# Pads of 64 bytes before and behind the pool of small tiles, in a two-block decoder kernel

## The chip, the cores and the metric

The kernel runs on one core of a Trainium2 chip. The metric is device time of one execution in microseconds; the median of several runs is compared. All inputs lie in the chip's main memory as float32 and are laid out by the host before the launch.

## The reference

Two transformer blocks over 256 tokens of width 1024, batch 1, all in float32. What matters here is that nearly all of it is matrix products, and that the largest part is the expert layer at the end of the second block:

```python
def second_block(x, mem, ...):
    ...
        x = x + peer_ffn(h, peer_w_q[l], peer_subkeys[l], peer_w_down[l], peer_w_up[l])
    return rmsnorm(x, final_g)

def peer_ffn(h, w_q, subkeys, w_down, w_up):
    ...
        q = (xc @ w_q).reshape(PEER_TOK_CHUNK, PEER_HEADS, 2, half).astype(jnp.float32)
        s = jnp.einsum("thpd,hpnd->thpn", q, subkeys.astype(jnp.float32))
        ...
        top_s, top_pos = lax.top_k(cand_s, PEER_TOPK)
        e = jnp.take_along_axis(cand_i, top_pos, axis=-1)
        g = jax.nn.softmax(top_s, axis=-1).astype(xc.dtype)
        a = jax.nn.gelu(jnp.einsum("td,thkd->thk", xc, w_down[e]))
        return jnp.einsum("thk,thkd->td", g * a, w_up[e])
```

Ahead of it stand the first block (a gated recurrence, a multi-scale pooling, a merge, a squared-ReLU MLP of width 4096, two layer norms) and the second block's attention, spatial gating and cross attention. There are 16,384 experts, so w_down and w_up of the expert layer are 64 MB each.

## The kernel before

**Products in split precision.** Every large product is done in float32r with both operands split in a high and a low part, and three matmuls for each pair: high x high, low x high, high x low. Two functions do nearly all of them. gemm_t (lines 195 to 223) keeps a 128x128 slice of the weights stationary and moves 256 columns of activations (all tokens), which gives a transposed result; its three matmuls are lines 207, 208 and 209. gemm_n (lines 226 to 296) keeps a 128x128 slice of the activations stationary (one half of the tokens) and moves 512 columns of weights, which gives a result with tokens on the partitions; its matmul is line 240.

**Weights.** They come as 128x1024 pieces (512 KB) by DMA, issued on SyncE's queue in one fixed order (`plan`), into tiles named raw. feed (line 134) makes the high part with ScalarE (line 152), low (line 159) the low part with VectorE (line 164: raw minus high). A piece with both parts is a tile w of pool spl (4 buffers, line 144), or wb in pool big, or a part of lend.

**The expert layer.** It computes all experts densely, in 16 groups of 1024. down(g) is a gemm_t of w_down with the normalised input h4, followed by a gelu into slots. route (line 1306) makes, from the routing weights, one-hot tables (tile oo, VectorE, lines 1330 to 1333), multiplies them on TensorE (tile gt, line 1339) and scales the activations in slots (line 1343). up(g, ...) (line 1373) multiplies the scaled activations with w_up into four PSUM banks py, which are kept over all 16 groups:

```python
            for n, (x, w) in enumerate(((wh, hi), (wl, hi), (wh, lo))):
                for h in which:
                    PE.matmul(yps[t][h], x[:, i % 2, tok(t)], w[:, h * 512:h * 512 + 512], ...
```

The stationary operand is a 128x128 slice of wh or wl, the moving one 512 columns of a weight piece. wh and wl are the split parts of two rows of slots, made by halves (line 1351) through split_to (lines 316 and 317).

**Where tiles lie.** Tiles are placed by pool, in the order in which pools are opened, each start rounded up to 32 bytes of the partition:

| pool, line | tiles that matter | first byte | start modulo 256 |
|---|---|---|---|
| keep, 36 | xh/xl, x1, h2, h3, h4 (high and low, 8192 bytes each) | 18,048 | 128 |
| raw, 37 | raw | 34,432 | 128 |
| sm, 38 | all of t2 (2048 bytes each), among them wh and wl; small statistics | 50,816 | 128 |
| spl, 42 | w | 67,392 | 64 |
| big, 46 | wb, and activations such as f0h to f3l, mh, ml, oh, ol; later lend and slots | 100,160 | 64 |

Slices that the matmuls use start at multiples of 512 bytes within a tile, so a slice has the residue of its tile.

**What sets the order.** TensorE, VectorE and ScalarE run in the order of the source; side work (the recurrence, attention, routing) is put between steps of the products by generators. The last pool's last tile, rt, ends at byte 229,184 of 229,376.

Of the kernel before, what the change touches and what calls it, by code (L numbers as in the profile page):

```python
# [8 lines left out]
F32 = mybir.dt.float32  # L9
# [8 lines left out]
P = 128  # L18
# [12 lines left out]
def kernel(ctx: ExitStack, tc: tile.TileContext, A: dict, out: bass.AP):  # L31
    nc = tc.nc
    V, S, G, PE = nc.vector, nc.scalar, nc.gpsimd, nc.tensor

    const = ctx.enter_context(tc.tile_pool(name="const", bufs=1))
    keep = ctx.enter_context(tc.tile_pool(name="keep", bufs=1))
    raw_p = ctx.enter_context(tc.tile_pool(name="raw", bufs=4))
    sm = ctx.enter_context(tc.tile_pool(name="sm", bufs=2))
    ps_n = ctx.enter_context(tc.tile_pool(name="ps_n", bufs=4, space=bass.MemoryType.PSUM))
    ps_p = ctx.enter_context(tc.tile_pool(name="ps_p", bufs=2, space=bass.MemoryType.PSUM))  # L40
    ps_s = ctx.enter_context(tc.tile_pool(name="ps_s", bufs=2, space=bass.MemoryType.PSUM))
    spl = ctx.enter_context(tc.tile_pool(name="spl", bufs=4))
    dram = ctx.enter_context(tc.tile_pool(name="dram", bufs=1, space=bass.MemoryType.DRAM))
    phase = ctx.enter_context(ExitStack())
# [1528 lines left out]
```

## Time and profile before

| | us |
|---|---|
| median of 3 runs | 1504.67 (1504.32 to 1505.53) |
| the profiled execution | 1504.66 |
| its span, first to last instruction | 1502.9 |
| TensorE busy with matmuls, of the span | 1465.1 |
| VectorE busy | 1084.0 |
| ScalarE busy | 714.4 |

The order of time is: first block to about 430 us, second block's mixer and cross attention to about 700 us, then the expert layer: down of 14 groups to 1071 us (with the routing beside it), up of two groups with the last two downs to 1161 us, up of the others to 1487 us, with the second routing beside it until about 1304 us, and a tail. A matmul's recorded length is longer than the time to the next one, since matmuls overlap; how often one starts is read from a stretch and its count.

### The profile page before, as it was taken

To read this page: it belongs to the slowest core of one execution; us is meant where nothing else is said; L and a number is where in the kernel's file an instruction comes from. 1 tells how busy PE (TensorE), PEld (TensorE's weight loads), DVE (VectorE), ACT (ScalarE), POOL (GpSimd) and SP (SyncE) were. 2 spreads that over 40 slices of the span, in tenths; PEclk is the share of its full clock that TensorE was granted. 3 is DMA by queue.
4 is the path that set the end of the run, shared out by engine and by line. 5 is a ranking of instruction groups with operands and counts; after the bars stand their busy time and mean duration, and the time that the engine had idled before them with its cause. 6 is when DMAs were issued, how large, how long until landed. Compare 5 with 4: busy or idle time off the path is not lost.

```text
span 1502.9 us, 25892 instructions
## 1 busy us (share of the span) xinstructions
PE 1465.1 (97%) x10408; PEld 1325.0 (88%) x10408; DVE 1084.0 (72%) x1932; ACT 714.4 (48%) x929; POOL 37.6 (3%) x70
## 2 busy tenths in 40 slices
PE   8999999999999999899999999999999999999997
PEld 8989997998877898778999999999999777788885
DVE  6876787565488679545998966888645999855555
ACT  5663354454453565444544544434444444444443
POOL 1004000000001000000000000000000000000001
PEclk9999999999999999999999999999999999999999
DMA  8554574466645455424456555555566555556552
GB/s 287 176 160 123 156 242 177 172 208 196 196 170 197 137 183 160 168 68 169 155 167 212 183 185 182 164 160 169 169 184 195 158 180 192 174 183 194 187 186 90
DMA packets 72761, 263.41 MB, mean 175 GB/s; under 512 B 8240, under 2 KB 8752, under 8 KB 72128
## 3 DMA queue, kind: packets, MB, share of 16 engines
q1 hardware_dynamic: 70416, 252.48, 52.7%
q0 software_dynamic: 1936, 8.98, 1.6%
q8 instruction: 82, 1.34, 0.4%
q14 instruction: 39, 0.32, 0.1%
q10 hardware_dynamic: 288, 0.30, 0.1%
HBM read 259.62 MB, written 2.10 MB: 174 GB/s over the span
## 4 chain that ended last, share of the span: by engine, by line
PE 93%; DVE 5%; ACT 1%; DMA 1%; issue 0%; SPq 0%; ACTq 0%; DVEq 0%
PE py L1381 24%; PE pt L207 16%; PE pt L208 16%; PE pn L240 16%; PE pt L209 16%; PE gt L1339 2%; DVE wb L164 1%; PE hs L625 1%; PE sk L1264 0%; DVE w L164 0%; PE tr L332 0%; PE tr L454 0%; DMA raw<-in_xa_o_dram 0%; DMA raw<-in_w_f_dram 0%; DVE rs_a L400 0%
## 5 line engine op out<-in xcount | busy, mean ns | idle before, releaser
L152 ACT ACTIVATE w<-raw 128x1024 fp32r<-128x1024 f32 (+1 forms) x416 | 436.1, 1050 | 583.6 <-PE pt L209 276.5
L164 DVE TENSOR_TENSOR w<-raw,w 128x1024 fp32r<-128x1024 f32 x410 | 499.0, 1221 | 168.6 <-ACT w L152 168.0
L207 PE MATMUL pt<-h4h,w 128*128 128x256 f32 x1088 | 307.4, 283 | 0.0
L208 PE MATMUL pt<-h4l,w 128*128 128x256 f32 x1088 | 304.6, 280 | 0.0
L209 PE MATMUL pt<-h4h,w 128*128 128x256 f32 x1088 | 303.7, 279 | 0.0
L1381 PE MATMUL py<-w,wh 128*128 128x512 f32 x1024 | 289.1, 398 | 0.0
L1381 PEld LDWEIGHTS py<-w,wh 128*128 128x128 f32 x1024 | 189.9, 188 | 43.4
L207 PEld LDWEIGHTS pt<-h4h,w 128*128 128x128 f32 x1088 | 204.7, 188 | 0.1
L208 PEld LDWEIGHTS pt<-h4l,w 128*128 128x128 f32 x1088 | 204.3, 188 | 0.1
L209 PEld LDWEIGHTS pt<-h4h,w 128*128 128x128 f32 x1088 | 203.7, 187 | 0.0
L1381 PE MATMUL py<-w,wl 128*128 128x512 f32 x512 | 161.5, 395 | 0.0
L1381 PEld LDWEIGHTS py<-w,wl 128*128 128x128 f32 x512 | 96.2, 188 | 22.9
L207 PE MATMUL pt<-xh,w 128*128 128x256 f32 x384 | 110.6, 288 | 5.3 <-ACT w L152 5.3
L209 PE MATMUL pt<-xh,w 128*128 128x256 f32 x384 | 108.7, 283 | 0.0
L208 PE MATMUL pt<-xl,w 128*128 128x256 f32 x384 | 108.7, 283 | 0.0
L317 DVE TENSOR_TENSOR wl<-slots,wh 128x512 fp32r<-128x512 f32 (+1 forms) x68 | 44.3, 658 | 80.7 <-ACT wh L316 80.7
L207 PEld LDWEIGHTS pt<-xh,w 128*128 128x128 f32 x384 | 73.2, 191 | 5.9 <-ACT w L152 5.6
L152 ACT ACTIVATE wb<-raw 128x1024 fp32r<-128x1024 f32 x62 | 62.8, 1048 | 33.0 <-DMA raw<-in_w_up_dram 10.5
L164 DVE TENSOR_TENSOR wb<-raw,wb 128x1024 fp32r<-128x1024 f32 x62 | 73.4, 1218 | 2.2 <-ACT wb L152 2.0
L208 PEld LDWEIGHTS pt<-xl,w 128*128 128x128 f32 x384 | 73.3, 191 | 0.4 <-DVE xl L317 0.2
L209 PEld LDWEIGHTS pt<-xh,w 128*128 128x128 f32 x384 | 73.1, 190 | 0.1
L1333 DVE TENSOR_TENSOR oo<-oo,rt 128x512 f16<-128x512 f16 x128 | 48.7, 421 | 2.2
(488 smaller groups left out, 2415.1 us busy)
## 6 DMA issues: line engine op xcount, KB each, us to landing
raw<-in_peer_down_dram SPq DMA_DIRECT2D x128, 512.0 KB, 3.6
raw<-in_peer_up_dram SPq DMA_DIRECT2D x128, 512.0 KB, 3.7
raw<-in_w_up_dram SPq DMA_DIRECT2D x32, 512.0 KB, 4.8
raw<-in_w_down_dram SPq DMA_DIRECT2D x32, 512.0 KB, 3.8
raw<-in_w_gb_dram SPq DMA_DIRECT2D x16, 512.0 KB, 4.0
raw<-in_w_ga_dram SPq DMA_DIRECT2D x16, 512.0 KB, 4.7
raw<-in_w_out_dram SPq DMA_DIRECT2D x16, 512.0 KB, 4.5
raw<-in_peer_q_dram SPq DMA_DIRECT2D x16, 512.0 KB, 5.0
```

Source lines behind the costliest of these rows:

```text
L152: S.activation(pc[:, 0, x], raw[:, x], AF.Copy)
L164: V.tensor_tensor(pc[:, 1, :], raw, f32(pc[:, 0, :]), OP.subtract)
L207: PE.matmul(o, hi[:, f:f + P], xh(b, k, ALL), start=(k == 0), stop=False)
L208: PE.matmul(o, hi[:, f:f + P], xl(b, k, ALL), start=False, stop=False)
L209: PE.matmul(o, lo[:, f:f + P], xh(b, k, ALL), start=False, stop=(k == nk - 1))
L240: PE.matmul(o, xx(k, t), ww[:, kk * n + h * 512:kk * n + h * 512 + 512], start=(k == 0 and i == 0), stop=(k == nk - 1 and i == 2))
L317: V.tensor_tensor(lo, src, f32(hi), OP.subtract)
L625: PE.matmul(ps[:, h, :], kk[:, h, tok(t)], qq[:, h, tok(t)], start=True, stop=True)
L1333: V.tensor_tensor(o2[:, i].rearrange("p t (a two) -> p t a two", two=2), q2, turn(1 + i, t0, n), OP.mult)
L1339: PE.matmul(ps[:, u, :], p1[:, u, :], p2[:, i, u, :], start=(i == 1), stop=(i == 2))
L1381: PE.matmul(yps[t][h], x[:, i % 2, tok(t)], w[:, h * 512:h * 512 + 512], start=(first and i == 0 and n == 0), stop=(last and i == 7 and n ...
```

## The change

Two tiles of 16 float32 per partition (64 bytes), edge and edge2, are placed in pools of their own, one between the pools raw and sm, one between sm and spl. Each is filled with zeros by a memset on GpSimd, and nothing reads it.

```diff
     raw_p = ctx.enter_context(tc.tile_pool(name="raw", bufs=4))
+    edge = ctx.enter_context(tc.tile_pool(name="edge", bufs=1)).tile([P, 16], F32, tag="edge", name="edge")
+    G.memset(edge, 0.0)
     sm = ctx.enter_context(tc.tile_pool(name="sm", bufs=2))
     ps_n = ctx.enter_context(tc.tile_pool(name="ps_n", bufs=4, space=bass.MemoryType.PSUM))
     ps_p = ctx.enter_context(tc.tile_pool(name="ps_p", bufs=2, space=bass.MemoryType.PSUM))
     ps_s = ctx.enter_context(tc.tile_pool(name="ps_s", bufs=2, space=bass.MemoryType.PSUM))
+    edge2 = ctx.enter_context(tc.tile_pool(name="edge2", bufs=1)).tile([P, 16], F32, tag="edge2", name="edge2")
+    G.memset(edge2, 0.0)
     spl = ctx.enter_context(tc.tile_pool(name="spl", bufs=4))
```

So sm moves by 64 bytes and every pool behind it by 128; keep and raw stay. Modulo 256, before and after:

| pool | before | after |
|---|---|---|
| keep (activations of the products) | 128 | 128 |
| sm (wh, wl among them) | 128 | 192 |
| spl, big (weights, other activations) | 64 | 192 |

The order of instructions is the same on every engine but GpSimd, where the two memsets stand ahead of the one of ident. GpSimd's program before, from the branch into the kernel on (ident is the identity matrix for transposes, epsb and iof are constants):

```order
L1569 UNCONDITIONAL_BRANCH
L383 MEMSET ident 128x128
L387 MEMSET epsb 128x1
L389 ISA
L389 IOTA iof 128x128
L384 AFFINE_SELECT ident<-ident 128x128
```

The same place after the change:

```order
L1573 UNCONDITIONAL_BRANCH
L39 MEMSET edge 128x16
L45 MEMSET edge_84 128x16
L387 MEMSET ident 128x128
L391 MEMSET epsb 128x1
L393 ISA
L393 IOTA iof 128x128
L388 AFFINE_SELECT ident<-ident 128x128
```

All that GpSimd does after the branch stands two instructions later; nothing else has moved.

## Rows read from the trace of the kernel before

**Rows 1.** The page: busy time of the engines, and the chain by line.

```profile
PE 1465.1 (97%) x10408; PEld 1325.0 (88%) x10408; DVE 1084.0 (72%) x1932; ACT 714.4 (48%) x929; POOL 37.6 (3%) x70
...
PE 93%; DVE 5%; ACT 1%; DMA 1%; issue 0%; SPq 0%; ACTq 0%; DVEq 0%
PE py L1381 24%; PE pt L207 16%; PE pt L208 16%; PE pn L240 16%; PE pt L209 16%; PE gt L1339 2%; DVE wb L164 1%; PE hs L625 1%; PE sk L1264 0%; DVE w L164 0%; PE tr L332 0%; PE tr L454 0%; DMA raw<-in_xa_o_dram 0%; DMA raw<-in_w_f_dram 0%; DVE rs_a L400 0%
```

**Rows 2.** Waits: total us, times, longest.

```profile
ACT w L152 <- PE py L1381: 178.4, 114, 2.6
```

**Rows 3.** Stretches: us, busy time and instructions by engine, clock, DMA share, GB/s.

```profile
core 0: us, PE busy (x) PEld busy (x) DVE busy (x) ACT busy (x) POOL busy (x), PEclk, DMA share, GB/s
346.00:429.00 83.00, 83.00 (x368) 68.73 (x367) 46.39 (x52) 37.89 (x39) 0.00 (x0) 1.00 0.67 209
691.00:696.00 5.00, 5.00 (x23) 4.05 (x22) 2.13 (x4) 3.23 (x5) 0.00 (x0) 1.00 0.94 338
742.00:823.00 81.00, 81.00 (x690) 81.00 (x689) 76.75 (x261) 41.78 (x50) 0.00 (x0) 1.00 0.59 186
202.00:223.00 21.00, 21.00 (x177) 21.00 (x176) 20.80 (x24) 14.14 (x17) 0.73 (x1) 1.00 0.86 300
1164.00:1304.00 140.00, 140.00 (x1024) 110.79 (x1023) 134.97 (x250) 58.11 (x66) 1.05 (x2) 1.00 0.54 174
1308.00:1487.00 179.00, 179.00 (x775) 144.30 (x772) 97.01 (x99) 83.22 (x96) 0.00 (x0) 1.00 0.57 179
```

**Rows 4.** The chain in time: start us, length us, what, count.

```profile
224.24 19.07 PE pn L240 x84
...
345.58 84.36 PE pn L240 x372
...
690.85 5.60 PE pn L240 x24
...
1071.75 22.40 PE py L1381 x96
...
1308.21 179.06 PE py L1381 x767
```

**Rows 5.** Groups by line and form: count, busy us, mean ns of one.

```profile
L1381 PE MATMUL py<-w,wh 128*128 128x512 f32 x1024 | 289.1, 398 | 0.0
L1381 PE MATMUL py<-w,wl 128*128 128x512 f32 x512 | 161.5, 395 | 0.0
...
L240 PE MATMUL pn<-w,xh 128*128 128x512 f32 x64 | 20.6, 398 | 0.0
L240 PE MATMUL pn<-w,f1h 128*128 128x512 f32 x56 | 17.6, 389 | 0.0
```

**Rows 6.** The chain in time in a short stretch of gemm_t with h2.

```profile
510.97 0.11 PE pt L208
511.08 0.11 PE pt L209
...
513.46 0.11 PE pt L209
```

**Rows 7.** GpSimd in order of time: start us, us, instruction.

```profile
0.95 0.10 POOL L387 MEMSET epsb<- 128x1 f32 x1
...
4.74 0.29 POOL L526 TENSOR_SCALAR_AFFINE_SELECT cm<-cm 128x128 f32<-128x128 f32 x1
```

**Rows 8.** The tile ident: ns min/median/max, first and last start in us.

```profile
L678 PE MATMUL hr<-ident,rs_y x16: 270/272/273, 131.7 to 186.8; 128*128 128x128 f32 x16
```

**Rows 9.** VectorE's groups for the low parts of the weights, columns as in rows 5.

```profile
L164 DVE TENSOR_TENSOR w<-raw,w 128x1024 fp32r<-128x1024 f32 x410 | 499.0, 1221 | 168.6 <-ACT w L152 168.0
L164 DVE TENSOR_TENSOR wb<-raw,wb 128x1024 fp32r<-128x1024 f32 x62 | 73.4, 1218 | 2.2 <-ACT wb L152 2.0
```

## The prediction

> **What bounds the kernel now.** I read the page first. TensorE is busy for 97% of the span and the chain of work that ended last is 93% PE; within the chain the expert up-projection (L1381) has 24%, gemm_t (L207 to L209) 48% and gemm_n (L240) 16% [rows 1]. So the rate at which these three kinds of matmul follow each other is the time. VectorE and ScalarE make the weights' two parts, and ScalarE waits for TensorE in the up-projection 114 times, 178.4 us in all [rows 2]: buffers come free when TensorE has read them, not the other way round. From 1308 to 1487 us VectorE is busy for 97.0 of 179 us, ScalarE for 83.2 and the DMA engines for 0.57 at 179 GB/s, while they gave 300 GB/s at 202 to 223 us [rows 3]: a faster TensorE finds its weights there.
>
> The second view is the chain in order of time, from which a pitch (time from one matmul to the next) is a piece's length over its count. All of gemm_n and the up-projection moves 512 columns past 128x128 weights of the same type, with the clock granted at 1.00, its 2.4 GHz level [rows 3]. Yet there are two pitches [rows 4]. Up-projection: 179.06 us / 767 = 233.5 ns and 22.40 / 96 = 233.3. gemm_n with h4 as the stationary operand: 5.60 / 24 = 233.3. gemm_n with the hidden activations f0 to f3: 84.36 / 372 = 226.8, and with the merged mixer output mh and ml: 19.07 / 84 = 227.0. What sorts them is where the stationary operand begins modulo 256 bytes. The moving weights (pools spl and big) begin at 64. f, mh and ml lie in big, at 64 too, and have the short pitch. h4 lies in keep and the expert activations' parts wh, wl in sm, both at 128, and have the long one. The rows by form agree: one matmul of gemm_n is 389 ns long with f1h, 398 with xh, and the up-projection's 398 and 395 [rows 5]. Equal residues are thus worth 233.4 - 226.8 = 6.6 ns per 512 columns.
>
> In gemm_t the roles are swapped: weights are stationary (64), activations move, 256 columns. A count of a stretch holds some two matmuls begun before its edge, so the pitch with h4 (128 against 64) is 81.00 / 688 = 117.7 ns and with oh, ol (64 against 64) 21.00 / 175 = 120.0 [rows 3]. Here it is the unequal pair that is faster, by 2.3 ns. This is what makes the change hard to foresee.
>
> **The change part by part.** Stated as stationary minus moving start modulo 256, the five kinds go as follows. Up-projection, 16 groups x 8 x 3 x 4 = 1536 matmuls: +64 becomes 0. gemm_n from keep, 528 matmuls: +64 becomes -64. gemm_t from keep, 1824 steps of k x 3 = 5472: -64 becomes +64. gemm_n and gemm_t with both operands in big or spl (672 and 528): 0 stays 0.
>
> Up-projection: 1536 x 6.6 ns = 10.1 us less, all on the path but for one stretch. From 1164 to 1304 us, where VectorE also makes the one-hot tables of the second routing, it is busy for 134.97 of 140 us [rows 3]. That stretch holds 1024 matmuls, about half of them (512) of the up-projection; they would give 3.4 us while VectorE has 5.0 us idle. I take nothing off, and hold 3.4 us as the bound.
>
> gemm_t from keep: the trace has no row at +64 with 256 columns. From below the bound is the short stretch at 510.97 to 513.46 us, 22 matmuls in 2.49 us or 113.2 ns [rows 6], with the very residues that give 117.7 elsewhere: 5472 x -4.5 = -24.6 us. From above it is a rule of sign: unequal at +64 costs 6.6 ns over equal in the 512-column rows, so 120.0 + 6.6 = 126.6, and 5472 x 8.9 = +48.7 us. I take 117.7 unchanged, because the nearest row is gemm_t's own: same code, same column count, operands 64 bytes apart before and after. That the row at 113.2 and the row at 117.7 share all residues also says that with 256 columns the residues alone don't fix the pitch.
>
> gemm_n from keep: unequal before and after. From above, 233.3 unchanged, 0 us, which I take for the same reason; from below, by the sign rule, 226.8 - 2.3 = 224.5, so 528 x -8.8 = -4.6 us.
>
> Two memsets of 64 bytes on POOL, ahead of the one that fills ident: a memset of 128x1 is 0.10 us there, so 0.2 us, and that row of POOL's work is done by 5.03 us [rows 7]. What hides them is that ident is first read by TensorE at 131.7 us [rows 8]; without that cover they cost the 0.2 us. The order on all other engines is as it was, and the sizes of all other tiles too. VectorE's and ScalarE's operands move with their pools; the parts of weights in spl and in big, with other sources, take 1221 and 1218 ns on VectorE [rows 9], so I count nothing, and a cost there would lie under TensorE's time except in the stretch from 1164 us.
>
> Sum against the profiled execution: 1504.66 (span 1502.9 and 1.8 around it; the median of the runs is 1504.67, so no correction), minus 10.1, plus 0, is 1494.6 us. Its own range: 1498.0 if VectorE keeps the 3.4 us, 1490.0 if gemm_n gains 4.6 as well; 1489 to 1498 rounded.
>
> **The rivals.** The first ends slower: the sign decides, not the distance. One rule covers all four steady pitches: over equal residues, +64 costs 6.6 ns (rows of 512 columns) and -64 saves 2.3 (rows of 256). The change turns gemm_t's sign from the good one to the bad one. The price is +48.7 for gemm_t, -10.1 for the up-projection, -4.6 for gemm_n: +34.0, or 1538.7 us; without gemm_n's gain 1543. It decides as soon as gemm_t's pitch grows by 10.1 us / 5472 = 1.8 ns. For it speaks that it is the simplest rule; against it that no row holds both signs at one column count, and that the two column counts disagree already in what unequal residues do.
>
> Second, gemm_t goes to 120.0 ns, the highest steady pitch that the trace shows for it: 5472 x 2.3 = +12.6, minus 10.1, or 1507.2 us. For it: any new residue may lose what the old one had. Against it: 120.0 is seen only with equal residues.
>
> Third, the change does nothing: 1504.7 us. It may be that the pool, not the residue, sorts the rows: sm and keep lie below 67,392 bytes, spl and big above, and the change leaves that so. Or the period may be 512: f, mh and the weights are equal modulo 512 as well, but after the change wh begins at 192 and w at 448 modulo 512, 256 apart, and no row has that distance. For it speaks that the trace can't tell 256 from 512; against it that the residues sort every row of 512 columns.
> The Trainium skill's page "TensorE: Matmul & The Clock Gate" (Part 2, step-by-step) says that TensorE reads its moving operand and its weights from SBUF through two independent ports, so that loading the next weights takes nothing from the running matmul. By that rule where the two begin should not matter, and the time would be this rival's 1504.7 us. The trace speaks against it with 226.8 and 233.3 ns for one shape [rows 4].
>
> Fourth, gemm_t falls into the pitch of 113.2 ns: -24.6 and -10.1, or 1470.0 us. For it speaks the one stretch of [rows 6]; against it that the long stretches stay at 117.7.
>
> **How the numbers follow.** Forecast (up-projection at 226.8 to 227, gemm_t as before) 0.45; slower by sign 0.28; gemm_t at 120.0 0.07; nothing 0.13; gemm_t at 113.2 0.07. About 0.2%, 3 us, is what a measurement of this kernel can tell from no change. Faster by more: 0.45 + 0.07 = 0.52. Within: 0.13 + 0.07 (1507.2 is 0.17% over) = 0.20. Slower: 0.28. The likeliest case's own range is 1489 to 1498. For 8 in 10 the sign case, with more than 0.2, must be inside: 1489 to 1543, which leaves out the 0.07 at 1470 and the edges of the two large cases.
>
> **What will show it.** Right: in the chain of after, the long piece of the up-projection with its 767 matmuls at about 174 us instead of 179.06, and those of 96 at 21.8 instead of 22.40; from 742 to 823 us still about 690 matmuls. The sign case: some 640 matmuls in such a stretch (81 us / 126.6 ns), and gemm_n from keep at 224 to 225. Nothing: up-projection pieces at 233 ns. If VectorE takes the gain back, the stretch of the second routing stays 140 us long with VectorE busy all through. A pitch of gemm_t that I have not priced, above 121 or below 113, would make the forecast wrong outright, as 5472 matmuls turn each ns into 5.5 us.

## The result, and the profile after

| | before | after |
|---|---|---|
| median of the runs, us | 1504.49 (4 runs, 1504.05 to 1505.53) | 1480.42 (4 runs, 1478.89 to 1480.96) |
| ratio | 1 | 0.9841, 95% interval 0.9828 to 0.9854 |
| profiled execution, us | 1504.66 | 1480.96 |
| its span, us | 1502.9 | 1479.0 |

The changed kernel is 24.1 us faster. The forecast was 1494.6 us with a range from 1489 to 1543: the direction was right, the size was too small, and the time lies 8.6 us below the range. The pages first: busy time by engine, then the chain that ended last, by engine and by line (to be set beside [rows 1]).

```profile
PE 1437.9 (97%) x10408; PEld 1306.9 (88%) x10408; DVE 1083.9 (73%) x1932; ACT 714.5 (48%) x929; POOL 38.4 (3%) x72
...
PE 78%; DVE 10%; ACT 1%; issue 1%; DMA 0%; ACTq 0%; DVEq 0%; SPq 0%
PE py L1385 23%; PE pn L244 14%; PE pt L211 12%; PE pt L213 12%; PE pt L212 12%; DVE w L168 2%; PE gt L1343 2%; DVE wb L168 1%; DVE slots L1177 1%; DVE slots L1175 1%; DVE slots L1180 1%; PE tr L336 0%; PE tr L458 0%; DMA raw<-in_xa_o_dram 0%; DVE rs_a L404 0%
```

TensorE does the same 10408 matmuls in 27.2 us less busy time; VectorE's and ScalarE's busy times are where they were. What is new is VectorE's share of the chain, 10% instead of 5%, with the routing's top-16 (L1175, L1177, L1180) and the low parts of the weights (L168) in it. Next the chain in order of time, with the pieces that answer to [rows 4] (start us, length us, what, count).

```profile
220.48 19.07 PE pn L244 x84
...
340.29 84.34 PE pn L244 x372
...
683.22 5.49 PE pn L244 x24
...
1056.20 21.77 PE py L1385 x96
...
1289.37 173.99 PE py L1385 x767
```

The two pieces of gemm_n whose operands both lie in big or spl have not moved (19.07 and 84.34 us). The up-projection has the short pitch: 173.99 us / 767 = 226.8 ns, and 21.77 / 96 = 226.8. gemm_n with h4 went from 5.60 to 5.49 us for 24, that is 228.8 ns. Now stretches of the span (columns as in [rows 3]):

```profile
733.00:816.00 83.00, 82.87 (x712) 82.16 (x712) 78.47 (x266) 43.30 (x51) 0.00 (x0) 1.00 0.57 185
816.00:876.00 60.00, 60.00 (x532) 60.00 (x531) 52.79 (x132) 31.31 (x37) 0.00 (x0) 1.00 0.61 193
876.00:912.00 36.00, 36.00 (x308) 36.00 (x308) 18.73 (x21) 16.14 (x19) 0.00 (x0) 1.00 0.59 189
1145.00:1285.00 140.00, 140.00 (x1032) 112.16 (x1031) 136.59 (x252) 60.22 (x69) 1.06 (x2) 1.00 0.53 177
```

All four run at a granted clock of 1.00, as before. The first three are gemm_t with h4, the same code with the same operands, and have three rates. With two matmuls in the count that began before the edge: 60.00 / 530 = 113.2 ns, 36.00 / 306 = 117.6 ns, and in the first 83.00 / 710 = 116.9 ns with TensorE idle for 0.13 us. The first is a mixture: up to 778 us the steps are 113.3 ns apart but for a few interruptions, and 117.8 ns behind. Before, such stretches had 117.7 [rows 3].

Matmul by matmul the two traces can be laid side by side, since the order on TensorE is the same. From the start of the first to the start of the last matmul of a stage, in us (the count is of gemm_t's or the up-projection's own matmuls; small products stand between them in some stages):

| stage (kind of matmul, count) | before | after | difference |
|---|---|---|---|
| gemm_t with x, 1152 in three stages | 161.15 | 157.69 | -3.46 |
| gemm_t with x1, 576 | 68.16 | 65.64 | -2.53 |
| gemm_t with h2, 480 in two stages | 64.40 | 63.13 | -1.27 |
| gemm_t with h4, 2880, the down-projection beside the routing (3450 with the one-hot and other small products) | 363.68 | 356.00 | -7.68 |
| gemm_t with h4, two stretches between pieces of the up-projection, 192 each | 22.50 each | 22.50 each | 0.00 |
| up-projection, two pieces of 96 | 22.17 each | 21.55, 21.53 | -1.25 |
| up-projection, the other 1344, with 512 one-hot products | 331.08 | 323.83 | -7.25 |

So gemm_t gave 14.9 us and the up-projection 8.5. The rest of the 23.9 us is gemm_n from keep (the stages of x, h2, h3 and h4 together -1.1, while that of x1 takes 1.0 more) and waits that moved both ways.

The pitch can be taken further apart: from the starts of consecutive matmuls in the trace, without the steps in which TensorE waited, in blocks of six. Before, 5258 of 5302 intervals of gemm_t from keep are at 118 ns and 40 at 113. After, 3251 of 5297 are at 113, 1592 at 118, and the mean is 114.84; the blocks between the two are all the first six steps behind an interruption, at 115.5 on the mean. It is not a smooth distribution: a stretch takes one of two pitches and holds it until something else comes between. The timeline of the changed kernel shows one such turn (start us, us, instruction):

```profile
874.93 0.28 PE L211 MATMUL pt<-h4h,w 128*128 128x256 f32 x1
875.04 0.28 PE L212 MATMUL pt<-h4l,w 128*128 128x256 f32 x1
875.15 0.28 PE L213 MATMUL pt<-h4h,w 128*128 128x256 f32 x1
875.27 0.49 PE L1258 MATMUL rt<-ident,slots 128*128 128x128 f32 x3
875.52 0.36 PE L211 MATMUL pt<-h4h,w 128*128 128x256 f32 x1
875.72 0.28 PE L212 MATMUL pt<-h4l,w 128*128 128x256 f32 x1
875.83 0.28 PE L213 MATMUL pt<-h4h,w 128*128 128x256 f32 x1
875.95 0.28 PE L211 MATMUL pt<-h4h,w 128*128 128x256 f32 x1
876.07 0.28 PE L212 MATMUL pt<-h4l,w 128*128 128x256 f32 x1
```

Steps of 0.11 us up to the three transposes of the routing (rt), and of 0.12 us behind them, until 912 us. What comes ahead of a stretch seems to matter, but does not fix its pitch: all 32 stretches that follow the one-hot products (gt) are at 113 after and at 118 before, those that follow the up-projection are at 118 in both, those that follow hs are 8 at 113 and 5 at 118 after, and 13 at 118 before.

### The profile page after: what moved, and what is told of

Same layout as the page of the kernel before. It is cut to its first block, busy times and chain, and to the rows that moved or that the text cites. A ratio compares the mean times of both kernels' runs of the same rounds, so it can differ in the third digit from the quotient of the medians.

```text
span 1479.0 us, 25894 instructions
## 1 busy us (share of the span) xinstructions
PE 1437.9 (97%) x10408; PEld 1306.9 (88%) x10408; DVE 1083.9 (73%) x1932; ACT 714.5 (48%) x929; POOL 38.4 (3%) x72
## 4 chain that ended last, share of the span: by engine, by line
PE 78%; DVE 10%; ACT 1%; issue 1%; DMA 0%; ACTq 0%; DVEq 0%; SPq 0%
PE py L1385 23%; PE pn L244 14%; PE pt L211 12%; PE pt L213 12%; PE pt L212 12%; DVE w L168 2%; PE gt L1343 2%; DVE wb L168 1%; DVE slots L1177 1%; DVE slots L1175 1%; DVE slots L1180 1%; PE tr L336 0%; PE tr L458 0%; DMA raw<-in_xa_o_dram 0%; DVE rs_a L404 0%
## 5 line engine op out<-in xcount | busy, mean ns | idle before, releaser
L168 DVE TENSOR_TENSOR w<-raw,w 128x1024 fp32r<-128x1024 f32 x410 | 499.3, 1222 | 156.0 <-ACT w L156 154.7
L1385 PE MATMUL py<-w,wh 128*128 128x512 f32 x1024 | 283.1, 392 | 0.0
L168 DVE TENSOR_TENSOR wb<-raw,wb 128x1024 fp32r<-128x1024 f32 x62 | 73.4, 1219 | 2.2 <-ACT wb L156 2.0
```

Source lines behind the costliest of these rows:

```text
L168: V.tensor_tensor(pc[:, 1, :], raw, f32(pc[:, 0, :]), OP.subtract)
```

## The experiments

Three numbers describe a kernel here: the bytes put in before keep (c), before sm (a) and before spl (b). Before has 0, 0, 0; the change has 0, 64, 64. They set the distance of the two operands' starts modulo 256, stationary minus moving: gemm_t from keep at a + b - 64, the up-projection at 64 - b, gemm_n from keep at 64 - a - b. The table has all of them; pitches are means over undisturbed intervals, in ns, each with its distance in brackets. Each ratio is against runs of the kernel before on the same chip, whose median was 1503.9 to 1504.8 us. The same code with both operands in big or spl, at distance 0 in every kernel, stays at 119.7 to 119.8 ns in gemm_t and 227.0 to 227.3 in gemm_n, though its pools move against keep and raw in most of these runs: the distance that counts is that of the matmul's own two operands.

| kernel | c, a, b | us, median | ratio to before, 95% | gemm_t | up-projection | gemm_n |
|---|---|---|---|---|---|---|
| before | 0, 0, 0 | 1504.49 | | 117.75 (-64) | 233.23 (+64) | 233.33 (+64) |
| after | 0, 64, 64 | 1480.42 | 0.9828 to 0.9854 | 114.84 (+64) | 227.56 (0) | 229.13 (-64) |
| e1_back64 | 0, 0, 64 | 1503.89 | 0.9984 to 1.0003 | 119.85 (0) | 227.61 (0) | 227.55 (0) |
| e2_front128 | 0, 128, 0 | 1488.63 | 0.9881 to 0.9914 | 114.96 (+64) | 233.21 (+64) | 229.20 (-64) |
| e3_back128 | 0, 0, 128 | 1482.71 | 0.9844 to 0.9879 | 114.63 (+64) | 228.89 (-64) | 229.28 (-64) |
| e4_shift64 | 64, 0, 0 | 1503.87 | 0.9988 to 1.0007 | 117.67 (-64) | 233.23 (+64) | 233.29 (+64) |
| e5_shift32_after | 32, 64, 64 | 1481.60 | 0.9838 to 0.9875 | 115.03 (+64) | 227.57 (0) | 229.27 (-64) |
| e6_back32 | 0, 0, 32 | 1499.98 | 0.996 to 0.998 | 116.81 (-32) | 233.16 (+32) | 233.10 (+32) |
| e7_front32_back64 | 0, 32, 64 | 1498.52 | 0.995 to 0.9975 | 118.30 (+32) | 227.62 (0) | 233.18 (-32) |
| e8_front96_back64 | 0, 96, 64 | 1495.33 | 0.9926 to 0.9963 | 117.89 (+96) | 227.58 (0) | 233.38 (-96) |
| e12_front48_back64 | 0, 64, 64 in effect | 1480.09 | 0.9824 to 0.9857 | 115.07 (+64) | 227.57 (0) | 229.51 (-64) |
| e9_front128_back64 | 0, 128, 64 (keep 32 lower) | 1501.09 | 0.9977 to 0.9996 | 118.83 (128) | 227.64 (0) | 232.35 (128) |

Three theories are told apart: A, the distance of the two starts decides, with its sign; B, the distance without its sign; C, the absolute place of one pool or one operand. The expectations of e9 to e12 give the letters A and B to theories of their own. The edits below are against the changed kernel, except where said.

**e1_back64: only the pad behind.** All distances become 0.

```diff
-    edge = ctx.enter_context(tc.tile_pool(name="edge", bufs=1)).tile([P, 16], F32, tag="edge", name="edge")
-    G.memset(edge, 0.0)
```

> Only the pad between sm and spl, 64 bytes: keep, sm, spl and big all begin at 128 modulo 256, so every product has equal residues. Theory of residues: up-projection at 227 ns (before 233.3), gemm_n from keep at 227, gemm_t from keep at 120.0 (before 117.7). Sum: -8.5 us for the up-projection as the changed kernel had it, some -3 for gemm_n, up to +12 for gemm_t: 1500 to 1507 us. Rival, that the pool and not the residue decides: nothing moves, 1504.5 us.

The time is that of before. That is a sum of two effects, not none: in the chain the long piece of the up-projection is as short as in the changed kernel, while in the stretch of gemm_t from 742 to 823 us there are 678 matmuls instead of 690, 81.00 / 676 = 119.8 ns.

```profile
1313.29 173.99 PE py L1383 x767
```

```profile
742.00:823.00 81.00, 81.00 (x678) 81.00 (x677) 77.17 (x266) 41.04 (x48) 0.00 (x0) 1.00 0.56 181
```

The up-projection gains 8.5 us; the stage of the down-projection loses 5.7, that of x1 1.3. Of the distances measured here, equal starts are the best for 512 columns and the worst for 256.

**e2_front128: 128 bytes in front, none behind.** gemm_t gets +64 and the up-projection keeps +64.

```diff
-    edge = ctx.enter_context(tc.tile_pool(name="edge", bufs=1)).tile([P, 16], F32, tag="edge", name="edge")
+    edge = ctx.enter_context(tc.tile_pool(name="edge", bufs=1)).tile([P, 32], F32, tag="edge", name="edge")
...
-    edge2 = ctx.enter_context(tc.tile_pool(name="edge2", bufs=1)).tile([P, 16], F32, tag="edge2", name="edge2")
-    G.memset(edge2, 0.0)
```

> Only a pad before sm, 128 bytes: spl and big at 192 as in the changed kernel, sm at 0. gemm_t from keep is at +64 as in the changed kernel, the up-projection stays at +64 as before. If gemm_t's part of the gain (some 15 us) hangs on its own residues: gemm_t mostly at 113.3 ns, up-projection at 233, 1488 to 1491 us. If gemm_t's gain came from the small tiles of sm lying with the weights: 117.8 ns and 1504 us.

This splits the gain: the up-projection's long piece is 179.06 us as before, and gemm_t and gemm_n alone bring 1488.63 us, by the ratio 0.9898 some 15 us below before. In the chain and in a stretch of the down-projection:

```profile
1289.84 179.06 PE py L1383 x767
```

```profile
830.00:890.00 60.00, 60.00 (x526) 60.00 (x525) 45.36 (x65) 31.46 (x36) 0.00 (x0) 1.00 0.60 195
```

**e3_back128: none in front, 128 behind.** sm stays where it was; gemm_t has +64 again, and the up-projection has its first run at -64.

```diff
-    edge = ctx.enter_context(tc.tile_pool(name="edge", bufs=1)).tile([P, 16], F32, tag="edge", name="edge")
-    G.memset(edge, 0.0)
...
-    edge2 = ctx.enter_context(tc.tile_pool(name="edge2", bufs=1)).tile([P, 16], F32, tag="edge2", name="edge2")
+    edge2 = ctx.enter_context(tc.tile_pool(name="edge2", bufs=1)).tile([P, 32], F32, tag="edge2", name="edge2")
```

> Only a pad behind sm, 128 bytes: gemm_t from keep at +64 as in the changed kernel, the up-projection at -64 instead of +64 before and 0 in the changed kernel. If distance decides with 512 columns: up-projection between 229 and 233 ns, like gemm_n from keep in the changed kernel (229.1 at -64), 1483 to 1490 us. If the sign decides, as the rival of the prediction had it: up-projection below 227, near 224, and 1476 to 1479 us.

The up-projection at -64 has 175.66 us / 767 = 229.0 ns, between 226.8 at 0 and 233.4 at +64. So the sign counts for 512 columns as it does for 256 (there 117.75 at -64 and 114.84 at +64), and theory B falls. The time, 1482.71 us, is just under the 1483 to 1490 that was expected for this case. The two stretches of 192 that lie between pieces of the up-projection took 21.67 us here instead of 22.50, as they entered at 113 ns. In e2, with the up-projection at +64 ahead of both, one of the two did so, so the work ahead does not settle it by itself. That gives back 1.7 of the 2.3 us that the up-projection lost, and the kernel stands within its interval of the changed one.

```profile
1287.71 175.66 PE py L1383 x767
```

**e4_shift64: everything 64 bytes on, against the kernel before.** The distances stay, the places change.

```diff
     const = ctx.enter_context(tc.tile_pool(name="const", bufs=1))
+    edge0 = ctx.enter_context(tc.tile_pool(name="edge0", bufs=1)).tile([P, 16], F32, tag="edge0", name="edge0")
+    G.memset(edge0, 0.0)
     keep = ctx.enter_context(tc.tile_pool(name="keep", bufs=1))
```

> A pad of 64 bytes before keep alone: keep and sm at 192, spl and big at 128. All differences are as in the kernel before, all absolute residues are moved by 64. If differences decide: 117.8 and 233.3 ns and 1504.5 us. If the absolute residue of an operand decides, gemm_t (activations at 192, weights at 128) or the up-projection moves by some ns, that is 8 us or more.

**e5_shift32_after: the changed kernel, everything 32 bytes on.**

```diff
     const = ctx.enter_context(tc.tile_pool(name="const", bufs=1))
+    edge0 = ctx.enter_context(tc.tile_pool(name="edge0", bufs=1)).tile([P, 8], F32, tag="edge0", name="edge0")
+    G.memset(edge0, 0.0)
     keep = ctx.enter_context(tc.tile_pool(name="keep", bufs=1))
```

> The changed kernel with a further pad of 32 bytes before keep: keep at 160, sm, spl and big at 224. All differences as in the changed kernel. If differences decide: gemm_t from keep mostly at 113.3 ns, up-projection at 227 to 228, 1480 us. If the absolute place counts for the new pitch of gemm_t: 117.8 ns and some 1495 us.

Neither shift does anything: 1503.87 us is before, 1481.60 is after, and every mean pitch is that of the kernel with the same distances to 0.2 ns. Theory C falls. Which stretch takes which of gemm_t's two pitches is not the same, though. This row of e5 has the long one, where the changed kernel has the short one (its 355 matmuls stand below, behind e8):

```profile
830.00:870.00 40.00, 40.00 (x342) 40.00 (x341) 34.91 (x57) 21.15 (x25) 0.00 (x0) 1.00 0.59 191
```

From 876 to 912 us it is the other way round. So one stretch alone tells little of a distance; the means over all of them do.

**e6_back32, e7_front32_back64 and e8_front96_back64: other distances.** Against the changed kernel, e6 has no front pad and a back pad of 8 columns (32 bytes); e7 a front pad of 8 columns; e8 one of 24, whose edit is shown.

```diff
-    edge = ctx.enter_context(tc.tile_pool(name="edge", bufs=1)).tile([P, 16], F32, tag="edge", name="edge")
+    edge = ctx.enter_context(tc.tile_pool(name="edge", bufs=1)).tile([P, 24], F32, tag="edge", name="edge")
```

> Only a pad of 32 bytes behind sm: gemm_t from keep at -32, up-projection and gemm_n from keep at +32. If the cost grows evenly with the distance: up-projection near 230.4 ns, gemm_t near 118.8, 1506 us (-4 for the up-projection, +6 for gemm_t). If only equal or unequal counts: 233.3 and 117.8 as before, 1504.5 us.

> Pads of 32 bytes before and 64 behind sm: up-projection equal as in the changed kernel (227 to 228 ns), gemm_t from keep at +32, gemm_n at -32. If gemm_t falls evenly from 119.85 at 0 to 114.8 at +64: near 117.3, 1491 us or so. If any positive distance opens the pitch of 113.3: 1480 us. If +32 stays at 120: 1501 us.

> Pads of 96 bytes before and 64 behind sm: up-projection equal, gemm_t from keep at +96, gemm_n at -96. If gemm_t goes on falling with the distance, or 113.3 is taken in more stretches: 112 to 114 ns, 1476 to 1480 us. If +64 is the best place: above 114.8 ns and above 1481 us.

With 512 columns +32, -32 and -96 all cost as much as +64 (233.1 to 233.4). With 256 columns +32 and +96 are at 118.3 and 117.9, both worse than the +64 between them, and -32 at 116.8 is a little better than -64. A slope between the measured points is out. Of the expectations the second of e8 came true, those of e6 and e7 did not: 1499.98 us where 1504.5 or 1506 was said, and 1498.52 where 1480, 1491 or 1501 was. In the same 40 us of the down-projection there are 342 matmuls before and in e4, 346 at -32, 340 at +32, 343 at +96, and 355 in the changed kernel; the rows are those of e6, e7, e8 and after, in this order:

```profile
830.00:870.00 40.00, 40.00 (x346) 40.00 (x345) 36.29 (x89) 21.58 (x26) 0.00 (x0) 1.00 0.60 190
```

```profile
830.00:870.00 40.00, 40.00 (x340) 40.00 (x339) 36.37 (x112) 21.05 (x24) 0.00 (x0) 1.00 0.59 183
```

```profile
830.00:870.00 40.00, 40.00 (x343) 40.00 (x342) 36.28 (x102) 21.34 (x25) 0.00 (x0) 1.00 0.60 187
```

```profile
830.00:870.00 40.00, 40.00 (x355) 40.00 (x355) 36.39 (x67) 21.83 (x26) 0.00 (x0) 1.00 0.63 197
```

**e10_before_light and e11_after_light: the routing with half of its top-16.** gemm_t gained 14.9 us and not the 24.6 that 113.2 ns everywhere would give. In the down-projection the chain of the changed kernel runs through VectorE, for some 60 us like this (start us, length us, what, count):

```profile
739.22 1.12 DVE w L168
740.34 0.39 DVE slots L1175 x2
740.73 0.52 DVE slots L1177 x2
741.25 0.52 DVE slots L1180 x2
...
742.69 1.12 DVE w L168
```

A turn of 3.47 us: the low part of one weight piece, 1.12 us, then a step of the top-16. A chain that can run through two engines that are both busy need not mean that the second one costs time. So both kernels were run with less on VectorE (the same edit in both; shown here as in the changed kernel):

```diff
-        for r in range(2):
-            c = slice(r * 8, r * 8 + 8)
-            for vals, idx, src in rows:
-                V.max(vals[:, c], src)
-            for vals, idx, src in rows:
-                V.max_index(idx[:, c], vals[:, c], src)
-            if r == 0:
-                for vals, idx, src in rows:
-                    V.match_replace(src, vals[:, c], src, LOWEST)
+        for vals, idx, src in rows:
+            V.max(vals[:, 0:8], src)
+        for vals, idx, src in rows:
+            V.max_index(idx[:, 0:8], vals[:, 0:8], src)
+        for vals, idx, src in rows:
+            V.tensor_copy(vals[:, 8:16], vals[:, 0:8])
+            V.tensor_copy(idx[:, 8:16], idx[:, 0:8])
```

> The kernel before, with the second half of the routing's top-16 left out: the best eight are found and copied to places 9 to 16 (so other experts are chosen; the work of TensorE and the weights read stay the same). VectorE loses some 17 us of the 78 that it works beside the 82.5 us stretch of the expert down-projection. Theory A (TensorE's own pitch of 117.7 ns sets that stretch before): the down-projection's 3450 matmuls of gemm_t stay at 363.7 us, within 1 us, and the time at 1503 to 1505 us. Theory B (VectorE already held TensorE there): the stretch shortens by 2 us or more.

> The changed kernel with the same half of the top-16 left out. Theory A (VectorE, held by the routing, takes back part of what gemm_t gains at 113.3 ns): the 3450 matmuls, 356.0 us in the changed kernel, fall to 352 to 353 us, VectorE goes from the chain there, and the time is 1476 to 1478 us. Theory B (the pitch alone, 113.3 or 117.8 ns by how a stretch was entered, sets it): 356 us, within 1 us, and 1479 to 1481 us.

Before does not notice: 1504.36 us, ratio 0.9994 to 1.0013, and the stage of the down-projection (3450 matmuls, of which 2880 are gemm_t's) takes 363.68 us, to the last digit what it took. The changed kernel does: the stage takes 353.44 us instead of 356.00. The whole came out at 1478.08 us (4 runs, 1476.87 to 1481.15) beside 1480.09 for e12 on the same chip; these 2 us lie within the spread of the runs. The stage is the sharper measure: in the five kernels with gemm_t at +64 and the whole routing (after, e2, e3, e5, e12) it takes 355.4 to 356.7 us. The rows for the stretches, e10 and then e11:

```profile
742.00:823.00 81.00, 81.00 (x691) 81.00 (x690) 65.30 (x187) 42.14 (x50) 0.00 (x0) 1.00 0.58 184
```

```profile
733.00:816.00 83.00, 83.00 (x735) 83.00 (x734) 69.40 (x194) 43.94 (x52) 0.00 (x0) 1.00 0.60 191
```

In the first, VectorE has 11.5 us less to do than in [rows 3] and TensorE does one matmul more. In the second it has 9.1 us less than in the changed kernel, and TensorE does 735 instead of 712: 83.00 / 733 = 113.2 ns. The waits say the same. In the changed kernel TensorE's loading of weights (PEld) waits four times for the low part from 733 to 816 us, the last time just ahead of 778.47 us; VectorE is on the chain for the 60 us up to there (us in total, times, longest):

```profile
PEld pt L213 <- DVE w L168: 0.8, 4, 0.3
```

Before, in e10 and in e11 no such wait is found in the down-projection, nor in e2, whose gemm_t held the long pitch beside the routing; in e11 VectorE is gone from the chain there. So VectorE, which was no limit at 117.7 ns, is one at 113.2. With less on VectorE the stage is 2.6 us shorter. The steps of TensorE around the four waits were 1.15 us of that; the rest is a stretch that entered the other pitch, and whether VectorE or chance chose it is not shown. The edge of the expectation (352 to 353) was missed by 0.4 us, that of the time (1476 to 1478) by 0.1.

**e12_front48_back64 and e9_front128_back64: around +64, and farther.**

```diff
-    edge = ctx.enter_context(tc.tile_pool(name="edge", bufs=1)).tile([P, 16], F32, tag="edge", name="edge")
+    edge = ctx.enter_context(tc.tile_pool(name="edge", bufs=1)).tile([P, 12], F32, tag="edge", name="edge")
```

> The change with the first pad of 48 bytes instead of 64: gemm_t at +48, up-projection at 0, gemm_n at -48. Theory A (only a start 64 past the other one gives the short pitch; so far +32 and +96 gave 118): gemm_t at 117 to 119 ns mean, 1496 to 1499 us. Theory B (a window around +64 that starts before +48): 115 ns, 1480 to 1483 us.

This run tells nothing about +48, whatever its time seems to say for its theory B. A tile's start is rounded up to 32 bytes, so a pad of 48 puts sm where one of 64 does, and the kernel is the changed one with a smaller memset. As a repeat it is of use: 1480.09 against 1480.42 us, the stage of the down-projection in 355.99 against 356.00. Distances between +32 and +64 weren't tried.

For e9 the front pad is 32 columns, and the unused tile epsb is taken out to make room, which moves keep 32 bytes down.

```diff
-    edge = ctx.enter_context(tc.tile_pool(name="edge", bufs=1)).tile([P, 16], F32, tag="edge", name="edge")
+    edge = ctx.enter_context(tc.tile_pool(name="edge", bufs=1)).tile([P, 32], F32, tag="edge", name="edge")
...
-    epsb = const.tile([P, 1], F32, name="epsb")
-    G.memset(epsb, RMS_EPS)
```

> Front pad of 128 bytes, back pad of 64, and the unused tile epsb left out to make room: gemm_t at +128, up-projection at 0, gemm_n at 128. Theory A (+64 is a place of its own, other distances give about 118): gemm_t at 117 to 119 ns, up-projection 227.6, 1494 to 1499 us. Theory B (the farther the two starts are apart, the better): gemm_t at 113.3 all through, 1470 to 1476 us.

1501.09 us: the up-projection has its gain (its long piece is 173.99 us), and gemm_t at 128 has 118.8 ns and takes most of it back. The pitch is in the 117 to 119 ns of its theory A, the time above the 1494 to 1499: that range was too low for 118.8, since 5472 matmuls at 4.0 ns over the changed kernel's 114.84 make 1502 us. "The farther the better" is out. The row:

```profile
830.00:890.00 60.00, 60.00 (x508) 60.00 (x508) 50.12 (x127) 30.56 (x36) 0.00 (x0) 1.00 0.58 186
```

No kernel here beats the changed one: e12 is the same kernel, e3 and e5 stand within their intervals of it, and e11 leaves work out.

## Why the prediction was right or wrong

**What bounds the kernel, and what sorts the pitches: right.** The rate of the matmuls was the time, and the starts modulo 256 sort them. e4 and e5 show that it is the distance of the two operands that counts, e2 that it acts on each kind by itself: there gemm_t and gemm_n move and the up-projection stays.

**The up-projection: right in mechanism, a little too large.** Forecast -10.1 us, measured -8.5; 226.8 ns in the long pieces is as forecast (173.99 us where "about 174" was said). The missing 1.6 us are in the stretch with the one-hot products. The prediction set aside up to 3.4 us there for VectorE, and VectorE is not in the chain of that stretch. What is there are pieces of 12 and 24 matmuls between the one-hot products, first before, then after:

```profile
1224.97 0.48 PE gt L1339 x16
1225.45 2.87 PE py L1381 x12
...
1228.81 5.67 PE py L1381 x24
```

```profile
1211.05 5.56 PE py L1385 x24
1216.62 0.48 PE gt L1343 x16
1217.10 2.84 PE py L1385 x12
```

A pair gains 0.11 + 0.03 = 0.14 us, and 16 pairs 2.2, where 576 matmuls at 6.6 ns would be 3.8. In the trace the first ten or so matmuls behind each batch of one-hot products run at 224 to 236 ns in turn, and only then at 226 to 227; behind gemm_t they are there after three or fewer. So behind the one-hot products the short pitch needs a run-up, and a piece of 12 is nearly all run-up.

**gemm_t from keep: this is the step that failed.** "I take 117.7 unchanged, because the nearest row is gemm_t's own." It measured 114.84 on the mean, 14.9 us on the path. The bounds around it (113.2 and 126.6 ns) held it, but the range took in the upper one alone. The row that said otherwise was on the page: [rows 6] showed that gemm_t has a second pitch at 113.2. The prediction read from it that "the residues alone don't fix the pitch", which is right, and did not ask the next question: whether the residues set how often each of the two pitches is entered. At -64 that is 40 intervals in 5302, at +64 3251 in 5297. That the operands are "64 bytes apart before and after" was used as if the sign did not count, while the first rival, further on, said it might. The mark set for being right would have hidden it, too: from 742 to 823 us "still about 690 matmuls" were expected, and the changed kernel has 694 there, because VectorE holds up the first part of that window and most of the second is at the long pitch.

**gemm_n from keep: taken unchanged, measured -4.2 ns.** 233.33 became 229.13; 528 x 4.2 ns = 2.2 us, of which some 1.1 us show in the stages, x1's left out. The lower bound of 224.5 came from the sign rule and is too low.

**The memsets and the other engines: right.** The memset of ident starts 0.09 us later, at 0.90 instead of 0.81 us, and VectorE and ScalarE are busy for as long as before.

**The rivals.** The sign decides: half of it is true and the other half is upside down. The two signs do differ, at both column counts, but +64 is gemm_t's best and not its worst distance. The rule joined rows of 512 and of 256 columns into one, and nothing joins them: equal starts give 227 of 227 to 233 at 512 columns, and 119.8 of 115 to 120 at 256. The 0.28 that it had, and the 1543 that it put on the range, pulled the range to the wrong side. gemm_t at 120.0 is what e1 measures, at distance 0 where the prediction had seen it. "Nothing happens" is refuted by the time, and the pool as the cause by e1 and e2: the same pools have other pitches when their distances change. With wh and w 256 apart modulo 512 the up-projection still has 226.8 ns in the changed kernel, so the period is not 512. The rule of the Trainium skill beside it ("TensorE: Matmul & The Clock Gate", Part 2, step-by-step: two independent read ports) is not enough to describe these float32r matmuls: the conclusion that the starts should not matter fails here, since the traces have 113.2, 117.7 and 119.8 ns for one shape, by the distance of the starts. gemm_t at 113.2, the rival with a chance of 0.07 and 1470.0 us, was nearest in its mechanism.

**Where the rest of that rival's gain is.** If all 2880 matmuls of gemm_t in the down-projection went from 117.75 to 113.3 ns, that would be 12.8 us; 7.7 were measured. 2.6 of the other 5.1 are gone in e11, with less work on VectorE: 1.15 are its four waits (eight steps of 2.06 us together instead of 0.91), and 1.4 are some 300 intervals more at 118 ns (about 755, in e11 452). VectorE had only 4.25 us idle in the 81.00 us from 742 us [rows 3]; the prediction weighed this limit for the stretch from 1164 us alone, and the price of this rival leaves it out. What is left, 2.5 us, is those 452 intervals with 204 in the first six steps behind an interruption. The two stretches of 192 that follow the up-projection keep their 118 ns, 1.7 us of the forecast rival. Why a stretch enters one pitch or the other was not settled, nor why +64 opens the short one.

## What to carry to other kernels

Where a stream of matmuls is the whole path, list for each kind the starts of its two operands modulo 256 bytes and its pitch, and treat signed distances and column counts that no row shows as unknown in both directions. A second steady pitch in a short stretch is a state that the kernel can reach more often: price it as such, and put it in the range. When a faster matmul is priced, find the engine beside it with the least idle time (here VectorE, at 95% of the stretch in [rows 3]) and the point at which it becomes the limit.

## What the runs showed of the hardware

- float32r matmuls of 128x128 with 512 columns: 226.8 ns with both operands' starts equal modulo 256, 229.0 at -64 (stationary minus moving), 232 to 233.4 at -32, -96, +32, +64 and 128. With 256 columns: 119.8 at 0, 118.8 at 128, 118.3 at +32, 117.9 at +96, 117.7 at -64, 116.8 at -32, and 114.6 to 115.1 at +64 as a mean of two pitches. Those at +96 and 128 are means of two as well (long stretches at 117.3 and 118.6, and at 118.6 and 120.0). Absolute places don't count (e4, e5).
- At 256 columns and +64 there are two steady pitches, 113.2 and 117.7 ns; at -64 there are the same two, the short one in 40 of 5302 intervals. A stretch takes one behind an interruption and holds it: three transposes at 875.27 us turned one into the other for the next 36 us.
- In the up-projection with equal starts, the short pitch is reached only some ten matmuls behind the one-hot products; until then the steps are 224 to 236 ns in turn. Behind gemm_t it is there after three or fewer.
